# Rotary loads split from their arithmetic, one attention fetch moved ahead of eight loads, and squares moved ahead of evictions in a hybrid decoder block on one core

## The chip, the cores and the metric

The kernel runs on one core of one Trainium2 chip. The metric is the device time of one execution in microseconds (us), as the median of several runs. Trace times count from the start of the span, which is the time from the first to the last instruction of one profiled execution.

The core has five engines with a queue of instructions each: TensorE (PE, matmuls), VectorE (DVE), ScalarE (ACT), GpSimd (POOL) and SyncE (SP, which here only issues loads). An engine works through its queue in order. Transfers go through 16 DMA engines.

## The reference

One decoder layer on a sequence of 1024 tokens, model width 1024, in float32. After a first RMSNorm a wide projection feeds two branches, a gated linear recurrence and a dilated window attention in three groups of four heads. They are merged, projected, normed, and followed by a SwiGLU feed-forward part of width 2816. The parts that the change touches are these:

```python
def rms_norm(x, g):
    y = xf * lax.rsqrt(jnp.mean(xf * xf, axis=-1, keepdims=True) + EPS)
    return (y * g.astype(jnp.float32)).astype(x.dtype)
...
def partial_rope(t, cos, sin):
    half = ROPE_DIM // 2
    t1 = t[..., :half]
    t2 = t[..., half:ROPE_DIM]
    return jnp.concatenate([t1 * cos - t2 * sin, t2 * cos + t1 * sin, t[..., ROPE_DIM:]], axis=-1)
...
    s = jnp.einsum('brnqhc,brnkhc->brnhqk', qb, kb)
    s = jnp.where(mask[None, None, :, None], s, NEG)
    m = jnp.max(s, axis=-1, keepdims=True)
    p = jnp.exp(s - m)
```

The rotary part turns the first 32 of 128 components of each query and key head, for 12 heads.

## The kernel before

**Arithmetic.** A float32 product is made of three matmuls, since each operand is split into a high and a low part: `split` writes the high part on ACT (`whi`, `hth`) and the low part, source minus high, on DVE (`wlo`, `htl`). The large projections save one product in eight by a Strassen-like scheme; a `Quad` makes four 512x512 blocks of a projection from seven products P1 to P7, which are interleaved quad by quad. `Quad.prep` loads a pair of weight tiles (`wraw`, two buffers), forms sums of them on GpSimd (`sa`, `sb`), and splits the first tile, `sa`, `sb`, and a half of the second tile (`w4h`, `w4l`). So the first buffer of a pair comes free early in a quad and the second when `w4l` is done, near its end. P6 and P7 use the split of `sa`.

**Order.** The code of one engine is mostly run in the order in which a scheduler placed it; `tc.issue_after(x)` keeps what stands in it behind x. `load` chains all loads on SP in the order of the program. In the first loop over quads (`q1`: gates, queries and keys, and the gates of the merge) a counter goes up at every step (`tick`), and a table `todo` runs functions at given ticks: sixteen units of the recurrence, from tick 15 on every eight ticks (`lru_a`, and `lru_b` four ticks later), and six rotary units from tick `ROPE0` = 146 on every `ROPED` = 5 ticks. Tiles for both come from the pool `b2`, with 10 buffers of 128x512.

**Start.** `x_load(h, j)` brings x transposed, half h of the tokens, for the products, and `row_load` brings the same rows in the other direction (`xn`), for the sums of squares. `squares` takes them on ACT (`sq`), four tiles for each half. `rates` makes the reciprocal root from them: `rs` on ACT, a few small steps and `dg` on DVE, and one matmul on PE (`prb`) that spreads it. `normed` scales x by it on DVE, in place. Meanwhile the first projection (`v0_mm`, banks `bk0` and `bk1` for the two halves) runs on x that is not yet scaled, and `v0_out` scales its rows when it evicts them on ACT (`vs`). `put` splits a part of x. Then `v_start` and `v_quad` make the other values from the scaled x.

**Rotary.** `rotate(g, u)` loads four tiles of a group and a half of the tokens (`rq1`, `rq2` from the stored queries and keys, `rcs`, `rsn` from the tables), takes four products, a difference and a sum, and stores two tiles from GpSimd. One of the products, `rm2`, is on GpSimd (L812), the rest on DVE.

**Attention start.** `fetch_qk(h, g)` loads the query and key tile of head h and group g. `scores` calls it if it was not called before. In the stretch where attention begins, the results of the recurrence (`ld`) are also loaded, eight tiles `lraw`, to be split into `lTh` (ACT) and `lTl` for the products `py`.

Of the kernel before, what the change touches and what calls it, by code (L numbers as in the profile page):

```python
# [12 lines left out]
OP = mybir.AluOpType  # L13
# [32 lines left out]
ROPE0, ROPED = 146, 5  # L46
# [16 lines left out]
def block(ctx, tc, a, out):  # L63
# [364 lines left out]
    def row_load(t):  # L428
        XN.append(sp.tile([128, 1024], F32, name="xn", bufs=4))
        load(XN[t], a["x"][128 * t:128 * t + 128, :])  # L430
# [5 lines left out]
    def rates(ss):  # L436
# [11 lines left out]
        for t in range(4):  # L448
            V.tensor_scalar(dg[:, t], ident, e[:, t:t + 1], None, op0=OP.mult)
# [46 lines left out]
    for j in range(4):  # L496
        x_load(1, j)
    for t in range(4, NT):
        row_load(t)
    V.tensor_scalar(gneg, gpos, -0.5, None, op0=OP.mult)  # L500
    bk0 = [ps("pv") for _ in range(4)]
    ss = [sp.tile([128, 4], F32, name=f"ss{h}") for h in range(2)]
    for j in range(4):
        if j == 0:
            w0_split(j)
            with tc.issue_after(last_dve[0].ins):
                put(0, j)
        else:
            put(0, j)
            w0_split(j)  # L510
        if j < 3:
            v0_mm(bk0, 0, j)
# [5 lines left out]
    for j in range(4):  # L518
        put(1, j)
    for t in range(4, NT):  # L520
        squares(t, ss[1])
    for j in range(4):
        normed(0, j, rb)
# [3 lines left out]
    v0_out(bk0, 0, r0)  # L527
# [4 lines left out]
    for j in range(4):  # L532
        normed(1, j, rb)
    for j in range(4):
        put(0, j)
# [265 lines left out]

    def rotate(g, u):

        c = slice(512 * u, 512 * u + 512)
        t1, t2, cs, sn, m1, m2 = (b2(n) for n in ("rq1", "rq2", "rcs", "rsn", "rm1", "rm2"))
        rows = [qkd[g, :, :, 16 * i:16 * i + 16, c].rearrange("h s p n -> (h s) p n") for i in range(2)]
        load(t1, rows[0])
        load(t2, rows[1])
        for s, t in ((0, cs), (1, sn)):
            load(t, rtd[g, s, :, c].unsqueeze(0).broadcast_to([8, 16, 512]))  # L810
        V.tensor_mul(m1, t2, sn)
        G.tensor_mul(m2, t1, sn)  # L812
        V.tensor_mul(t1, t1, cs)
        V.tensor_mul(t2, t2, cs)
        V.tensor_sub(t1, t1, m1)
        V.tensor_add(t2, t2, m2)
        G.dma_start(rows[0], t1)
        G.dma_start(rows[1], t2)
# [11 lines left out]
    for n in range(6):  # L830
        todo.setdefault(ROPE0 + ROPED * n, []).append((rotate, (n // 2, n % 2)))
# [287 lines left out]

    for k in range(KT):  # L1120
        load(lraw[k], ld[k])
# [466 lines left out]
```

## Time and profile before

| | |
|---|---|
| runs, median of 3 | 1753.15 us (1753.12 to 1754.28) |
| profiled execution | 1749.78 us |
| its span | 1748.0 us |
| mean granted PE clock | 0.978 of full |
| PE busy | 1676.7 us, 96% of the span |
| DVE busy | 1113.9 us, 64% |
| ACT busy | 727.5 us, 42% |
| POOL busy | 698.0 us, 40% |
| DMA | 262.70 MB, mean 150 GB/s |

The profiled execution is a little longer than its span, by what lies before the first and after the last instruction. Busy times of different engines overlap; an engine's idle time costs something only where the engine that sets the end waits for it. The granted clock is the share of full speed that PE was given; a busy PE at a low clock does less.

### The profile page before, as it was taken

The page shows a single profiled execution, that of the slowest core. Times are in us where ns is not written, and L with a number is a line of the kernel's source. Part 1 is how long each engine was busy: PE and PEld are TensorE (multiplying, and loading weights), DVE is VectorE, ACT ScalarE, POOL GpSimd, SP SyncE. Part 2 cuts the span into 40 slices and gives each one's busy share as a digit, 9 for nine tenths or more (in the row PEclk, how much of TensorE's full clock was granted, in tenths as well). Part 3 has the DMA queues.
Part 4 walks back from the last instruction along what each step waited for, and adds up shares of the span by engine and source line. Part 5 has one row for each costly group of instructions (what it writes and reads, how often), then busy time and mean ns, then how long its engine had stood idle before and what let it go on. Part 6 is the DMA issues. An engine that isn't in the chain of part 4 may idle for free.

```text
span 1748.0 us, 21093 instructions
## 1 busy us (share of the span) xinstructions
PE 1676.7 (96%) x7748; PEld 1376.2 (79%) x7748; DVE 1113.9 (64%) x1585; ACT 727.5 (42%) x1130; POOL 698.0 (40%) x650
## 2 busy tenths in 40 slices
PE   8999999999999988989999999799999999999996
PEld 6897888787877876878888887678888888788885
DVE  6966676778788665563433577755545555649658
ACT  6423367554555522464451345422222222344343
POOL 2003354554445434214334204576556566400103
PEclk9899999999999999999999999899999999999998
DMA  8233433333333455584618742133222222475353
GB/s 319 73 133 113 148 133 124 135 137 129 127 133 133 139 166 179 197 330 155 229 50 304 269 162 84 49 115 133 102 103 91 103 91 103 150 261 198 109 186 121
DMA packets 95919, 262.70 MB, mean 150 GB/s; under 512 B 13768, under 2 KB 22120, under 8 KB 94408
## 3 DMA queue, kind: packets, MB, share of 16 engines
q1 hardware_dynamic: 70352, 182.49, 30.7%
q0 software_dynamic: 20352, 76.21, 11.5%
q10 hardware_dynamic: 5112, 2.66, 0.5%
q8 instruction: 61, 1.00, 0.2%
q14 instruction: 42, 0.34, 0.1%
HBM read 180.86 MB, written 80.35 MB: 149 GB/s over the span
## 4 chain that ended last, share of the span: by engine, by line
PE 77%; DVE 8%; DMA 5%; issue 4%; POOL 3%; ACT 2%; SPq 1%; ACTq 0%; DVEq 0%; POOLq 0%
PE pq L135 14%; PE pq L134 14%; PE pq L133 14%; PE pd L1334 4%; PE pd L1335 4%; PE pd L1333 4%; DMA rsn<-rtd 3%; PE py L135 2%; PE py L134 2%; PE py L133 2%; PE pv L463 2%; PE po L1017 2%; PE pv L133 1%; PE pv L135 1%; PE pv L134 1%
## 5 line engine op out<-in xcount | busy, mean ns | idle before, releaser
L135 PE MATMUL pq<-hth,wlo 128*128 128x512 f32 x448 | 179.7, 401 | 9.8 <-DVE wlo L99 9.8
L133 PE MATMUL pq<-hth,whi 128*128 128x512 f32 x448 | 179.6, 401 | 2.8 <-ACT whi L98 2.8
L134 PE MATMUL pq<-htl,whi 128*128 128x512 f32 x448 | 180.7, 403 | 0.0
L267 POOL TENSOR_TENSOR sb<-wraw 128x512 f32<-128x512 f32 x50 | 71.6, 1432 | 173.1 <-DMA wraw<-in_w_fg 92.3
L98 ACT ACTIVATE whi<-sa 128x1024 fp32r<-128x1024 f32 x50 | 53.0, 1059 | 201.5 <-PE pq L134 126.8
L1334 PE MATMUL pd<-fbl,fah 128*128 128x512 f32 x304 | 119.7, 394 | 4.5 <-DVE fbl L99 4.5
L1335 PE MATMUL pd<-fbh,fal 128*128 128x512 f32 x304 | 119.7, 394 | 0.0
L1333 PE MATMUL pd<-fbh,fah 128*128 128x512 f32 x304 | 119.3, 393 | 0.0
L98 ACT ACTIVATE whi<-wraw 128x1024 fp32r<-128x1024 f32 x67 | 70.7, 1055 | 98.2 <-PE pq L134 25.8
L135 PEld LDWEIGHTS pq<-hth,wlo 128*128 128x128 f32 x448 | 86.0, 192 | 32.1 <-DVE wlo L99 11.6
L99 DVE TENSOR_TENSOR wlo<-wraw,whi 128x1024 fp32r<-128x1024 f32 x67 | 91.6, 1367 | 26.4 <-ACT whi L98 23.7
L309 DVE TENSOR_TENSOR uw<-pq,uw 128x512 f32<-128x512 f32 x100 | 68.3, 683 | 60.2 <-PE pq L135 59.5
L133 PEld LDWEIGHTS pq<-hth,whi 128*128 128x128 f32 x448 | 86.0, 192 | 24.7 <-ACT whi L98 3.2
L134 PEld LDWEIGHTS pq<-htl,whi 128*128 128x128 f32 x448 | 85.9, 192 | 20.5
L1407 POOL TENSOR_TENSOR y<-y,gpf 128x512 f32<-128x512 f32 x16 | 25.2, 1602 | 186.9 <-ACT fah L98 109.5
L99 DVE TENSOR_TENSOR wlo<-sa,whi 128x1024 fp32r<-128x1024 f32 x50 | 70.1, 1401 | 28.6 <-ACT whi L98 28.6
L1239 POOL TENSOR_TENSOR fo<-fo,ut 128x512 f32<-128x512 f32 x44 | 60.6, 1381 | 67.1 <-DVE ut L1238 67.1
L720 DVE TENSOR_TENSOR fb<-pq,uw 128x512 f32<-128x512 f32 x84 | 67.8, 807 | 29.4 <-PE pq L135 29.0
L99 DVE TENSOR_TENSOR fal<-ar,fah 128x1024 fp32r<-128x1024 f32 (+1 forms) x41 | 50.5, 1231 | 51.5 <-ACT fah L98 51.4
L98 ACT ACTIVATE fah<-ar 128x1024 fp32r<-128x1024 f32 (+1 forms) x41 | 40.8, 995 | 100.9 <-PE pd L1334 79.5
L133 PE MATMUL pq<-t1h,whi 128*128 128x512 f32 x200 | 79.6, 398 | 0.9 <-ACT whi L98 0.9
L134 PE MATMUL pq<-t1l,whi 128*128 128x512 f32 x200 | 79.4, 397 | 0.0
(542 smaller groups left out, 4948.0 us busy)
## 6 DMA issues: line engine op xcount, KB each, us to landing
ar<-fd SPq DMA_DIRECT2D x35, 512.0 KB
qkd<-fb POOLq DMA_DIRECT2D x24, 512.0 KB, 3.6
qk<-qkd SPq DMA_DIRECT2D x24, 512.0 KB
wraw<-in_w_fg SPq DMA_DIRECT2D x24, 512.0 KB
wraw<-in_w_fu SPq DMA_DIRECT2D x24, 512.0 KB
fd<-fo POOLq DMA_DIRECT2D x11, 1024.0 KB, 4.3
wd<-in_w_dn SPq DMA_DIRECT2D x21, 512.0 KB
fd<-fs POOLq DMA_DIRECT2D x11, 768.0 KB, 5.6
```

What stands on the lines that cost most here:

```text
L98: A.activation(hi, src, AF.Copy)
L99: (le or V).tensor_sub(lo, src, f(hi))
L133: T.matmul(o, lh, rh, start=(first and i == 0), stop=False)
L134: T.matmul(o, lh, rl, start=False, stop=False)
L135: T.matmul(o, ll, rh, start=False, stop=(last and i == n - 1))
L267: G.tensor_add(sb[:, lo_], r1[:, lo_], r1[:, hi_])
L309: V.tensor_add(y, bank, x)
L720: V.tensor_add(o, half_in(bank, g), half_in(add, g))
L1239: G.tensor_mul(g, g, ut)
L1333: T.matmul(o, ah[:, ts], bh, start=(i == 0), stop=False)
L1334: T.matmul(o, ah[:, ts], bl, start=False, stop=False)
L1335: T.matmul(o, al[:, ts], bh, start=False, stop=(i == NP - 1))
```

## The change

There are three parts. In the start, the last two x loads of the second half stand behind the last four row loads, the second half's `squares` stand ahead of two of its four `put`, and `v0_out` of the first half is kept behind the second half's `rs`. In the first loop, `rotate` is split: `rotate_load` issues the four loads one unit, 5 ticks, ahead of the arithmetic; `ROPE0` goes from 146 to 148, so that loads stand at ticks 143, 148, ... 168 and the arithmetic at 148, 153, ... 173, where both stood at 146, 151, ... 171; and `m2` is on DVE. In the attention start, `fetch_qk(0, 2)` is called ahead of the eight `lraw` loads.

```diff
-ROPE0, ROPED = 146, 5
+ROPE0, ROPED = 148, 5
...
-            V.tensor_scalar(dg[:, t], ident, e[:, t:t + 1], None, op0=OP.mult)
+            last_dve[0] = V.tensor_scalar(dg[:, t], ident, e[:, t:t + 1], None, op0=OP.mult)
...
-    for j in range(4):
+    for j in range(2):
         x_load(1, j)
     for t in range(4, NT):
         row_load(t)
+    for j in range(2, 4):
+        x_load(1, j)
...
-            put(0, j)
-            w0_split(j)
+            with tc.issue_after(last_dve[0].ins):
+                put(0, j)
+                w0_split(j)
...
-    for j in range(4):
+    for j in range(2):
         put(1, j)
     for t in range(4, NT):
         squares(t, ss[1])
+    with tc.issue_after(last_act[0].ins):
+        for j in range(2, 4):
+            put(1, j)
     for j in range(4):
         normed(0, j, rb)
     bk1 = [ps("pv") for _ in range(4)]
     v0_mm(bk1, 1, 0)
     r1, rb = rates(ss[1])
-    v0_out(bk0, 0, r0)
+    with tc.issue_after(last_act[0].ins):
+        v0_out(bk0, 0, r0)
...
-    for j in range(4):
-        normed(1, j, rb)
-    for j in range(4):
-        put(0, j)
+    with tc.issue_after(last_dve[0].ins):
+        for j in range(4):
+            normed(1, j, rb)
+        for j in range(4):
+            put(0, j)
...
+    def rotate_load(g, u):
+
+        c = slice(512 * u, 512 * u + 512)
+        t = RT[g, u] = [b2(n) for n in ("rq1", "rq2", "rcs", "rsn")]
+        for i in range(2):
+            load(t[i], qkd[g, :, :, 16 * i:16 * i + 16, c].rearrange("h s p n -> (h s) p n"))
+        for i in range(2):
+            load(t[2 + i], rtd[g, i, :, c].unsqueeze(0).broadcast_to([8, 16, 512]))
+
     def rotate(g, u):
...
+        t1, t2, cs, sn = RT.pop((g, u))
+        m1, m2 = b2("rm1"), b2("rm2")
         V.tensor_mul(m1, t2, sn)
-        G.tensor_mul(m2, t1, sn)
+        V.tensor_mul(m2, t1, sn)
...
     for n in range(6):
+        todo.setdefault(ROPE0 + ROPED * (n - 1), []).append((rotate_load, (n // 2, n % 2)))
         todo.setdefault(ROPE0 + ROPED * n, []).append((rotate, (n // 2, n % 2)))
...
+    fetch_qk(0, 2)
     for k in range(KT):
         load(lraw[k], ld[k])
```

The order of ACT at the start, from the first half's `rs` on. `sq` are the squares, `vs` the evictions of the first half, `hth` the copies of `put`. Before:

```order
L425 ACTIVATE hth1_121<-x_125 128x2x512
L479 ACTIVATE vs0_393<-pv_167,rr4_287 128x512
L434 ACTIVATE sq_333,ss1_172<-xn_158 128x1024
L479 ACTIVATE vs0_393<-pv_168,rr4_287 128x512
L434 ACTIVATE sq_335,ss1_172<-xn_160 128x1024
L479 ACTIVATE vs0_393<-pv_169,rr4_287 128x512
L434 ACTIVATE sq_337,ss1_172<-xn_162 128x1024
L479 ACTIVATE vs0_393<-pv_170,rr4_287 128x512
L434 ACTIVATE sq_339,ss1_172<-xn_164 128x1024
L425 ACTIVATE hth0_120<-x_128 128x2x512
L439 ACTIVATE rs4_377<-ss1_172,epsc_87 128x4
```

After the change:

```order
L434 ACTIVATE sq_329,ss1_172<-xn_156 128x1024
L434 ACTIVATE sq_331,ss1_172<-xn_158 128x1024
L425 ACTIVATE hth0_120<-x_128 128x2x512
L434 ACTIVATE sq_333,ss1_172<-xn_160 128x1024
L425 ACTIVATE hth0_120<-x_129 128x2x512
L434 ACTIVATE sq_335,ss1_172<-xn_162 128x1024
L425 ACTIVATE hth1_121<-x_124 128x2x512
L439 ACTIVATE rs4_377<-ss1_172,epsc_87 128x4
L479 ACTIVATE vs0_393<-pv_167,rr4_287 128x512
L425 ACTIVATE hth1_121<-x_125 128x2x512
```

The evictions moved behind `rs`, and two `hth` copies of the scaled first half (x_128, x_129) stand between the squares.

The order of SP in the first rotary quads: `wraw` are a quad's two weight tiles, the four tiles from `rq1` to `rsn` a rotary unit. Before:

```order
L109 DMA wraw_4993<-in_w_g 128x1024
L109 DMA wraw_4995<-in_w_g 128x1024
L109 DMA rq1_5034<-qkd_1410 128x1x512
...
L109 DMA rsn_5037<-rtd_117 128x1x512
L109 DMA rq1_5144<-qkd_1410 128x1x512
...
L109 DMA rsn_5147<-rtd_117 128x1x512
L109 DMA wraw_5166<-in_w_g 128x1024
L109 DMA wraw_5168<-in_w_g 128x1024
L109 DMA rq1_5254<-qkd_1410 128x1x512
```

After the change:

```order
L109 DMA rq1_4961<-qkd_1410 128x1x512
...
L109 DMA rsn_4964<-rtd_117 128x1x512
L109 DMA wraw_5001<-in_w_g 128x1024
L109 DMA wraw_5003<-in_w_g 128x1024
L109 DMA rq1_5082<-qkd_1410 128x1x512
...
L109 DMA rsn_5085<-rtd_117 128x1x512
L109 DMA wraw_5156<-in_w_g 128x1024
L109 DMA wraw_5158<-in_w_g 128x1024
L109 DMA rq1_5207<-qkd_1410 128x1x512
```

The first unit moved ahead of a pair of weight tiles, the second behind it; the third stands behind the next pair in both, now with the fourth unit behind it.

The order of DVE in the second of these quads, from the low part of its first weight tile to that of `sa`. Before:

```order
L99 TENSOR_TENSOR wlo_5177<-wraw_5166,whi_5176 128x1024
L811 TENSOR_TENSOR rm1_5258<-rq2_5255,rsn_5257 128x512
L309 TENSOR_TENSOR uw_5205<-pq_5192,p1_5142 128x512
L813 TENSOR_TENSOR rq1_5254<-rq1_5254,rcs_5256 128x512
...
L816 TENSOR_TENSOR rq2_5255<-rq2_5255,rm2_5259 128x512
L309 TENSOR_TENSOR uw_5220<-pq_5207,uw_5205 128x512
L720 TENSOR_TENSOR fb_5162<-pq_5222,uw_5220 128x512
L99 TENSOR_TENSOR wlo_5181<-sa_5170,whi_5180 128x1024
```

After the change:

```order
L99 TENSOR_TENSOR wlo_5167<-wraw_5156,whi_5166 128x1024
L825 TENSOR_TENSOR rm1_5307<-rq2_5208,rsn_5210 128x512
L309 TENSOR_TENSOR uw_5195<-pq_5182,p1_5150 128x512
L826 TENSOR_TENSOR rm2_5308<-rq1_5207,rsn_5210 128x512
...
L830 TENSOR_TENSOR rq2_5208<-rq2_5208,rm2_5308 128x512
L728 TENSOR_TENSOR fb_5152<-pq_5230,uw_5228 128x512
L825 TENSOR_TENSOR rm1_5417<-rq2_5318,rsn_5320 128x512
L99 TENSOR_TENSOR wlo_5171<-sa_5160,whi_5170 128x1024
```

The third unit stands at the same place; the product of GpSimd joined it, and the first product of the fourth unit stands ahead of `wlo` of `sa`.

## Rows read from the trace of the kernel before

**Rows 1.** The page's first part: busy us, share of the span, instructions.
```profile
PE 1676.7 (96%) x7748; PEld 1376.2 (79%) x7748; DVE 1113.9 (64%) x1585; ACT 727.5 (42%) x1130; POOL 698.0 (40%) x650
```

**Rows 2.** Windows of 10 us: busy us and instructions by engine, clock, DMA share, GB/s.
```profile
30.00:40.00 10.00, 9.79 (x43) 7.59 (x41) 7.76 (x11) 7.86 (x15) 1.66 (x2) 1.00 0.59 231
40.00:50.00 10.00, 3.26 (x6) 1.96 (x7) 7.77 (x16) 3.62 (x4) 0.00 (x0) 0.62 0.55 191
```

**Rows 3.** Timeline of PE: start, duration, instruction, idle before it and releaser.
```profile
27.64 1.02 PE L451 MATMUL prb<-dg,ones 128*128 128x512 f32 x2
...
46.74 2.04 PE L451 MATMUL prb<-dg,ones 128*128 128x512 f32 x2 [6.95 <-DVE dg L449]
...
78.45 0.28 PE L133 MATMUL pv<-whi,hth 128*128 128x256 f32 x1
```

**Rows 4.** Timeline of ACT at the start.
```profile
32.14 0.69 ACT L479 ACTIVATE vs<-pv,rr 128x512 f32<-128x512 f32 x1 [5.28 <-PE pv L463]
32.73 1.05 ACT L434 ACTIVATE sq<-xn 128x1024 f32<-128x1024 f32 x1
...
39.55 0.29 ACT L439 ACTIVATE rs<-ss,epsc 128x4 f32<-128x4 f32 x1
```

**Rows 5.** Timeline of DVE at the start.
```profile
45.73 0.86 DVE L449 TENSOR_SCALAR dg<-cst,re 128x128 f32<-128x128 f32 x4
48.82 5.36 DVE L457 SCALAR_TENSOR_TENSOR x<-x,gneg,prb 128x512 f32<-128x512 f32 x8 [2.23 <-PE prb L451]
...
74.44 1.21 DVE L550 TENSOR_TENSOR htl<-x,hth 128x1024 fp32r<-128x1024 f32 x1
75.58 1.21 DVE L621 TENSOR_TENSOR wlo<-wraw,whi 128x1024 fp32r<-128x1024 f32 x1
```

**Rows 6.** Waits of DVE, 600 to 700 us: total, times, longest.
```profile
DVE rm L811 <- DMA rsn<-rtd: 36.3, 6, 9.0
```

**Rows 7.** Waits of PE, 600 to 700 us: total, times, longest.
```profile
PE pq L135 <- DVE wlo L99: 9.8, 4, 4.7
```

**Rows 8.** Timeline of DVE in the rotary stretch.
```profile
612.88 0.69 DVE L811 TENSOR_TENSOR rm<-rq,rsn 128x512 f32<-128x512 f32 x1 [6.37 <-DMA rsn<-rtd]
...
620.27 0.69 DVE L811 TENSOR_TENSOR rm<-rq,rsn 128x512 f32<-128x512 f32 x1 [2.40 <-DMA rsn<-rtd]
...
641.72 1.82 DVE L811 TENSOR_TENSOR rm<-rq,rsn 128x512 f32<-128x512 f32 x1 [9.04 <-DMA rsn<-rtd]
...
647.87 1.21 DVE L99 TENSOR_TENSOR wlo<-sa,whi 128x1024 fp32r<-128x1024 f32 x1
```

**Rows 9.** Timeline of PE in the rotary stretch.
```profile
649.13 0.80 PE L135 MATMUL pq<-hth,wlo 128*128 128x512 f32 x1 [4.68 <-DVE wlo L99]
649.73 0.63 PE L133 MATMUL pq<-hth,whi 128*128 128x512 f32 x1
...
653.14 0.53 PE L135 MATMUL pq<-hth,wlo 128*128 128x512 f32 x1
...
674.56 0.79 PE L135 MATMUL pq<-hth,wlo 128*128 128x512 f32 x1 [3.68 <-DVE wlo L99]
```

**Rows 10.** Timeline of SP's DMA issues in the rotary stretch.
```profile
612.94 16.14 SPq L109 DMA_DIRECT2D wraw<-in_w_g  x2
629.25 1.29 SPq L109 DMA_DIRECT2D rq<-qkd  x2
```

**Rows 11.** Line L812 by itself: count, shortest, median and longest ns, first and last start.
```profile
L812 POOL TENSOR_TENSOR rm<-rq,rsn x6: 1291/1760/1811, 612.9 to 691.0; 128x512 f32<-128x512 f32 x6
```

**Rows 12.** Timeline of PE at the attention start.
```profile
762.71 0.55 PE L901 MATMUL psc<-qk 128*128 128x128 f32 x1 [5.53 <-DMA qk<-qkd]
```

**Rows 13.** Timeline of SP's DMA issues at the attention start.
```profile
740.19 10.59 SPq L109 DMA_DIRECT2D lraw<-ld  x8
750.82 0.93 SPq L109 DMA_DIRECT2D qk<-qkd  x2
```

More of the change, by code (lines that the diff above doesn't have):

```diff
@@ L800, in lru_b @@
         G.dma_start(ld[cb, :, 512 * u:512 * u + 512], i)
-    def rotate(g, u):
[L804 to L810, printed above, removed]
+    RT = {}
+    def rotate_load(g, u):
[5 more added lines that the diff above has]
+            load(t[2 + i], rtd[g, i, :, c].unsqueeze(0).broadcast_to([8, 16, 512]))
+    def rotate(g, u):
+        t1, t2, cs, sn = RT.pop((g, u))
+        m1, m2 = b2("rm1"), b2("rm2")
         V.tensor_mul(m1, t2, sn)
-        G.tensor_mul(m2, t1, sn)
+        V.tensor_mul(m2, t1, sn)
         V.tensor_mul(t1, t1, cs)
@@ L816, in rotate @@
         V.tensor_add(t2, t2, m2)
-        G.dma_start(rows[0], t1)
-        G.dma_start(rows[1], t2)
+        c = slice(512 * u, 512 * u + 512)
+        for i, t in enumerate((t1, t2)):
+            G.dma_start(qkd[g, :, :, 16 * i:16 * i + 16, c].rearrange("h s p n -> (h s) p n"), t)
     def late_rates():
```

## The prediction

> **What bounds the kernel now.** I read the page first: TensorE (PE) is busy for 1676.7 of 1748.0 us [rows 1], so only what stops PE, or slows its clock, costs time. I then looked for the stops in the three stretches that the change touches, with the PE timeline, the chain of waits by engine, and the timeline of the engine that PE waited for.
>
> In the first 80 us the reader is to see one stop: PE stands 6.95 us before the second `prb` matmul, for VectorE's (DVE's) `dg` [rows 3]. The chain behind it starts on ScalarE (ACT): the `vs` evictions wait 5.28 us for PE, the four `sq` of the second half stand among them, and `rs` comes at 39.55 [rows 4]; on DVE `dg` ends at 46.59 [rows 5]. After the stop PE runs slow: in the window 40 to 50 us the granted clock is 0.62, with PE busy 3.26 us, against 43 matmuls in the 10 us before, 0.23 us each, at full clock [rows 2].
>
> In the rotary stretch (600 to 700 us) DVE waits 36.3 us, six times, for the sine table `rsn` of a rotary unit [rows 6], and PE waits 9.8 us, four times, for the `wlo` that stands behind this on DVE [rows 7]. Only the second number costs time, with what the clock loses behind it: after the stop of 4.68 us nine matmuls (649.73 to 653.14) start 0.43 apart instead of 0.23 [rows 9], so the clock is at half, and some 2.0 us are lost with the one before them; after the stop of 3.68 I put 2.8. So some 14.6 us hang on the rotary part.
>
> In the attention start PE waits 5.53 us for the `qk` tile of head 0, group 2 [rows 12], whose loads SyncE (SP) issues at 750.82, behind eight `lraw` loads issued from 740.19 for 10.59 us [rows 13].
>
> **Start-up.** The squares move ahead of the evictions, so `rs` and `dg` no longer wait for PE. By the order on ACT the last `sq` now follows two `put` copies that need DVE's first four `normed` steps, so `rates(1)` is not free at once. With 1.05 us per ACT pass of 128x1024 [rows 4] and DVE's unchanged `normed` steps I place the second `prb` at about 40, where PE has just finished what it had (about 39.6): the wait of 6.95 nearly goes. With the slow clock behind it (`prb` 2.04 against 1.02 the first time [rows 3], some eight matmuls by 0.2 as in [rows 9]) PE gains about 9.6 us up to there.
> But DVE does not gain as much. From `prb` on it has eight `normed` steps (5.36 us [rows 5]), then, by the order, 21 passes of 128x1024 at 1.14 us (74.44 to 75.58 [rows 5]) and two of 0.6 before the `wlo` for `v_quad`'s first product is done: 31.6 us, against 28.0 before (48.82 to 76.79 [rows 5]), since three `htl` and one `wlo` that stood ahead of `dg` now stand behind it. From 41 that ends at 72.6. PE began this product at 78.45 [rows 3]. It would be there at about 69.5, so a new wait of some 3 us opens, and with it a slow stretch of about 1.5 us, as behind the other stops. Six matmuls of 256 columns, 0.12 us each as half of the 0.23, go ahead of the wait. Net: 78.45 - 72.6 + 0.7 - 1.5 = 5.0 us gained. Bounds: 9.6 if DVE's passes prove to have slack, 3.0 if `prb` comes 2 us later. I take **5.0**: the DVE passes stand end to end in this stretch, so their sum counts.
>
> **The moved x loads.** Two x loads go behind four `xn` loads. The transfers are the same; the two x tiles are needed later than the squares now. Nothing, covered by the passes above.
>
> **Rotary.** Three things change. The product `m2` moves from GpSimd (1.29 to 1.81 us, median 1.76 [rows 11]) to DVE (0.69 us, as its twin at 612.88 [rows 8]): six times 0.6 us more on DVE, but the detour over GpSimd goes, worth about 1.1 us per unit that stands on the path. The arithmetic comes two ticks later, the loads three ticks earlier.
> What counts is where loads and arithmetic stand now. On SP each unit's four loads still come in line with the `wraw` pairs; before the change two `wraw` issue from 612.94 for 16.14 us (the second waits for its buffer until the quad's end) and the unit's loads come right behind, at 629.25 [rows 10], so that `rsn` serves DVE at 641.72, 12.5 us later [rows 8]. By the order of the changed kernel, unit 0 alone gets ahead of its `wraw` pair. Units 1, 2, 4 and 5 are still issued right behind a second `wraw`, and on DVE their first product still stands right behind the next `wlo`. These waits of DVE stay. What goes is the second unit inside a quad: before the change unit 1 is waited for again at 620.27, 2.40 us [rows 8], which pushes everything behind it, and with it the next second `wraw`. So I walk through the quads:
> - First (unit 1 alone): no stop. Its tail is about 4.5 us earlier, so the next second `wraw` is issued near 624.5 instead of 629.
> - Second (units 2 and 3): unit 2's `rsn` lands near 637.5, its arithmetic ends near 641; unit 3 lands some 6 us behind it. `wlo` of `sa` at about 645 instead of 647.87 [rows 8], where PE needs it at 644.2 (649.13 less 4.68 [rows 9], less the 0.2 of the first quad). Stop about 1 instead of 4.68, no slow clock.
> - Third (unit 4 alone): PE is here some 6.5 us earlier, DVE's wait for unit 4 only 3: stop about 3 instead of 3.68, slow stretch 2 to 2.7.
> - Fourth (unit 5): stop about 1.5, as before.
> Sum: 5.5 us of stops and 2.6 of slow clock are left of 14.6: **6.5** gained. Bounds: 14.6 if the waits fall away altogether, 0 or a little under if unit 3's landing just takes over the stop at `sa` (then 2.5 with what the third quad saves).
>
> How long a unit takes to land decides this. The row is 12.5 us from issue to use [rows 8, 10]. The Trainium skill, page "DMA: Bandwidth & Descriptors", section "Anatomy of one DMA — SWDGE (gpsimd) path", gives about 2.0 us plus the bytes over 436 GB/s, for transfers that GpSimd issues. By it the second `wraw` and a unit, 1.5 MB, would land in an estimated 5.6 us, DVE would hardly wait, and the sum would be that of the first rival below, about 1734. The trace disagrees by a factor of two for these loads.
>
> **Attention.** The two `qk` loads of group 2 now stand ahead of the eight `lraw`; their buffers come free with the first scores of head 0, near 743. So the wait of 5.53 goes from there. But the `lraw` loads start 3 us later than 740.19 and have 1 MB ahead of them, and by the order on ACT three of the eight `lTh` copies, instead of one, now stand behind the softmax of the first groups. PE runs the scores early and then stands before the products of the last `lTh`. I take **0.5 lost**; bounds 6 gained (the wait and its slow clock go whole) and 3 lost (the delay of `lraw` shows whole).
>
> **Sum.** 5.0 + 6.5 - 0.5 = 11.0 us of the span of 1748.0, so 1737.0. The profiled execution took 1749.78, and the median of the runs, 1753.15, is 3.4 above that; the difference is taken over: **1742.2**. No change means within 0.2%, 3.5 us.
>
> **The rivals.**
> - *Rotary loads really lead* (0.14). Every unit's data is there when DVE comes. For it: that is what an issue five ticks ahead does if a tick is long. Against: the order on SP, where the second `wraw` is still the gate. 14.6 + 5.0 - 0.5: 1734.
> - *DVE is not the next limit at the start* (0.13): the 9.6 us stay whole. For it: GpSimd and ACT could be late too, and DVE's work need not be in time everywhere. Against: DVE's passes without a gap. 15.6 gained: 1737.5.
> - *The rotary change does nothing* (0.15): the loads move with the arithmetic, the same waits end last, only one unit later. Left are 5.0 - 0.5: 1748.7.
> - *Slower* (0.06): SP, which issues in order, stands at a unit's loads for a buffer (a unit takes four of a pool of ten, and its two temporaries come on top), and the `wraw` pair behind it is late. Place: units 1, 3 and 5. Each us past the time at which the second `wraw` was free to go is a us for PE. At 4.5 us in three quads it costs 13.5, less 4.5: 1762. It decides from 1.5 us a quad. Against: four, two and four fit into ten, and the tiles freed are those of work some 20 us old.
> - *Little anywhere* (0.04): rotary as the third, and `prb` late: about 1751.
>
> **How the numbers follow.** The forecast has 0.48. Faster by over 0.2%: 0.48 + 0.14 + 0.13 and two thirds of the third rival, 0.85. Within 0.2%: the rest of that and the last, 0.09. Slower: 0.06. The range goes from the first rival, 1733, to a little past the third, 1750.
>
> **What would show it.** Right: the second `prb` near 40 with hardly a wait, and a new wait for `wlo` near 70; DVE waits of 6 to 9 us for `rsn` for units 1, 2, 4, 5; PE stops of about 1, 3 and 1.5 us in quads two to four; no wait for `qk` of group 2, but waits for `lTh` behind it. Wrong: no new wait near 70, or `rsn` not among DVE's waits (then nearer 1734), or SP late at `wraw` (then slower).

## The result and the profile after

The changed kernel takes 1736.59 us (median of 4 runs, 1734.92 to 1740.01) against 1753.72 us for the kernel before, measured beside it (4 runs, 1753.12 to 1761.02): ratio 0.9897, 95% interval 0.987 to 0.9923. It is faster, by 1.0%. The forecast was 1742.2, with a range of 1733 to 1750. The profiled execution took 1737.8 us with a span of 1736.0; the span was forecast as 1737.0. So the span's difference, 12.0 us against the 11.0 forecast, was closer than the medians' difference, 17.1 us: the profiled execution of before lay 3.4 below the median of its three runs, that of the changed kernel 1.2 above its own, and I had carried the 3.4 over as if it belonged to the kernel. By the medians alone the two faster rivals, 1734 and 1737.5, came nearer than the forecast; only the traces can tell which mechanism was at work.

The page's first part after the change; PE has the same work in a shorter span:

```profile
PE 1676.3 (97%) x7748; PEld 1376.8 (79%) x7748; DVE 1121.0 (65%) x1591; ACT 728.4 (42%) x1130; POOL 693.2 (40%) x644
```

To see where the 12 us came from I set each matmul of one trace beside the same matmul of the other and took the difference of their starts. A matmul that starts 5.5 us earlier at 590 us tells that 5.5 us were won up to there; it stands as -5.5. All times at the head of a column are those of the kernel before; the entries are the difference at that matmul.

| span's differences to the kernel before, us | 60 | 590 | 705 | 800 | 1734 |
|---|---|---|---|---|---|
| changed kernel | -11.7 | -5.5 | -16.2 | -12.4 | -12.0 |

So the start-up wins 11.7 and gives 6.2 of it back, the rotary stretch wins 10.6, and the attention start gives 3.7 back (16.13 at 735 to 12.42 at 800). Other executions of the same code give other numbers, as the experiments show below.

**Start-up.** The windows of 10 us (compare [rows 2]): the hole between 40 and 50 us is gone, at full clock, and a smaller one opens behind 60, with the granted clock at 0.83 behind it.

```profile
40.00:50.00 10.00, 10.00 (x45) 8.02 (x44) 10.00 (x13) 1.10 (x2) 0.00 (x0) 1.00 0.22 70
50.00:60.00 10.00, 10.00 (x64) 9.01 (x63) 10.00 (x9) 6.29 (x8) 1.45 (x2) 1.00 0.42 150
60.00:70.00 10.00, 7.85 (x65) 7.43 (x63) 9.79 (x11) 8.85 (x12) 0.09 (x1) 1.00 0.17 58
70.00:80.00 10.00, 9.20 (x64) 9.20 (x65) 8.80 (x10) 2.00 (x2) 0.70 (x1) 0.83 0.35 107
```

PE's timeline (compare [rows 3]): the second `prb` waits 0.69 us at 37.78 instead of 6.95 at 46.74. New waits of 1.76 and 1.19 us stand before `v_quad`'s first product.

```profile
9.99 2.03 PE L463 MATMUL pv<-wlo,hth 128*128 128x512 f32 x8
...
37.78 1.10 PE L451 MATMUL prb<-dg,ones 128*128 128x512 f32 x2 [0.69 <-DVE dg L449]
...
69.09 0.51 PE L133 MATMUL pv<-whi,hth 128*128 128x256 f32 x2 [1.76 <-ACT whi L628]
70.80 0.39 PE L134 MATMUL pv<-wlo,hth 128*128 128x256 f32 x1 [1.19 <-DVE wlo L629]
```

The first of these rows shows what I had not forecast: the kernel before waited here, in the row that the next fence quotes from its PE timeline, for DVE's first `wlo`. In the changed kernel that matmul runs at 9.99 without a wait.

```profile
12.18 2.07 PE L463 MATMUL pv<-wlo,hth 128*128 128x512 f32 x7 [2.09 <-DVE wlo L420]
```

On DVE (compare [rows 5]) the chain behind `prb` stands end to end, as forecast, and its `wlo` ends at 70.75:

```profile
38.92 5.36 DVE L457 SCALAR_TENSOR_TENSOR x<-x,gneg,prb 128x512 f32<-128x512 f32 x8
...
69.53 1.22 DVE L629 TENSOR_TENSOR wlo<-wraw,whi 128x1024 fp32r<-128x1024 f32 x1
```

**Rotary.** The waits of DVE (580 to 700 us) and of PE (590 to 700 us), total, times, longest (compare [rows 6, 7]): DVE still waits nearly as long for `rsn`, and PE stops once, for 3.1 us, instead of four times for 9.8.

```profile
DVE rm L825 <- DMA rsn<-rtd: 32.2, 5, 9.8
```

```profile
PE pq L135 <- DVE wlo L99: 3.1, 1, 3.1
```

PE's timeline at this stop shows what it costs besides: eight matmuls, from 661.98 to 664.96, start 0.43 us apart instead of 0.23, so the clock is at half for them, and some 1.6 us go to it.

```profile
661.17 0.50 PE L135 MATMUL pq<-hth,wlo 128*128 128x512 f32 x1 [3.14 <-DVE wlo L99]
...
661.98 0.63 PE L135 MATMUL pq<-hth,wlo 128*128 128x512 f32 x1
662.40 0.63 PE L133 MATMUL pq<-hth,whi 128*128 128x512 f32 x1
...
665.38 0.40 PE L134 MATMUL pq<-t1l,whi 128*128 128x512 f32 x1
```

DVE's timeline (compare [rows 8]) has the waits of units 1, 2, 3 and 4, and `wlo` of `sa` behind them:

```profile
606.66 0.83 DVE L825 TENSOR_TENSOR rm<-rq,rsn 128x512 f32<-128x512 f32 x1 [5.67 <-DMA rsn<-rtd]
...
627.84 0.69 DVE L825 TENSOR_TENSOR rm<-rq,rsn 128x512 f32<-128x512 f32 x1 [7.24 <-DMA rsn<-rtd]
...
634.58 0.69 DVE L825 TENSOR_TENSOR rm<-rq,rsn 128x512 f32<-128x512 f32 x1 [1.24 <-DMA rsn<-rtd]
635.18 1.22 DVE L99 TENSOR_TENSOR wlo<-sa,whi 128x1024 fp32r<-128x1024 f32 x1
...
654.49 0.69 DVE L825 TENSOR_TENSOR rm<-rq,rsn 128x512 f32<-128x512 f32 x1 [9.81 <-DMA rsn<-rtd]
```

The issues of SP (compare [rows 10]) show the same pattern as before, a unit right behind the second weight tile, but the second tile goes 10.36 us after the first instead of 16.14:

```profile
606.97 10.36 SPq L109 DMA_DIRECT2D wraw<-in_w_g  x2
617.43 1.24 SPq L109 DMA_DIRECT2D rq<-qkd  x2
```

From its issue at 617.43 to its use at 627.84 unit 2 takes 10.4 us, less than the 12.5 us of the kernel before. The estimate of 5.6 us, worked out from the Trainium skill's page "DMA: Bandwidth & Descriptors" (section "Anatomy of one DMA — SWDGE (gpsimd) path", for transfers that GpSimd issues), is again too short for these loads, which SP issues.

**Attention start.** The wait of 5.53 us [rows 12] is gone; PE stops four times instead, for 7.5 us by these rows of its timeline. Behind the last of them the product of the softmax (`po`) waits 0.41 us more for `pts`, the transposed probabilities that ACT copies.

```profile
747.72 0.50 PE L134 MATMUL py<-lTl,whi 128*128 128x512 f32 x1 [1.72 <-DVE lTl L99]
749.18 0.50 PE L134 MATMUL py<-lTl,whi 128*128 128x512 f32 x1 [0.50 <-DVE lTl L99]
...
756.39 0.50 PE L133 MATMUL py<-lTh,whi 128*128 128x512 f32 x1 [2.07 <-ACT lTh L98]
...
767.21 1.54 PE L917 MATMUL psc<-qk 128*128 128x128 f32 x8 [3.18 <-DMA qk<-qkd]
```

SP (compare [rows 13]) issues the moved fetch at 727.31 and the `lraw` loads behind it from 728.16. The kernel before issued them at 740.19, which less the 16.1 us won by then is 724.1: they start 4.1 us late.

### The profile page after: what moved, and what is told of

The parts are those of the page before. It is cut to its first block, busy times and chain, and to the rows that moved or that the text cites. A ratio compares the mean times of both kernels' runs of the same rounds, so it can differ in the third digit from the quotient of the medians.

```text
span 1736.0 us, 21088 instructions
## 1 busy us (share of the span) xinstructions
PE 1676.3 (97%) x7748; PEld 1376.8 (79%) x7748; DVE 1121.0 (65%) x1591; ACT 728.4 (42%) x1130; POOL 693.2 (40%) x644
## 4 chain that ended last, share of the span: by engine, by line
PE 77%; DVE 10%; DMA 4%; issue 4%; POOL 3%; ACT 3%; SPq 0%; ACTq 0%; DVEq 0%; POOLq 0%
PE pq L135 15%; PE pq L134 15%; PE pq L133 15%; PE pd L1351 4%; PE pd L1352 4%; PE pd L1350 4%; PE py L135 2%; PE py L133 2%; PE py L134 2%; PE pv L463 2%; PE po L1033 2%; PE pv L134 1%; PE pv L135 1%; DMA rsn<-rtd 1%; PE pv L133 1%
## 5 line engine op out<-in xcount | busy, mean ns | idle before, releaser
L99 DVE TENSOR_TENSOR wlo<-wraw,whi 128x1024 fp32r<-128x1024 f32 x67 | 97.5, 1456 | 23.6 <-ACT whi L98 20.8
L268 POOL TENSOR_TENSOR sa<-sb,wraw 128x512 f32<-128x512 f32 x50 | 80.2, 1604 | 0.0
```

The costliest lines, as they stand in the source:

```text
L99: (le or V).tensor_sub(lo, src, f(hi))
L268: G.tensor_sub(sa[:, lo_], sb[:, lo_], r0[:, lo_])
```

## The experiments

Each is named by its label. "Without the fetch" is the changed kernel without its attention fetch (`no_fetch`), the base of most of them. The table has the same differences as above, to the kernel before, in each kernel's profiled execution, and the ratio of the times measured.

| kernel | 590 | 705 | 735 | 800 | 1734 | ratio to before (95%) |
|---|---|---|---|---|---|---|
| start_only | -7.9 | -7.1 | -7.0 | -6.8 | -4.2 | 0.9968 (0.995 to 0.9986) |
| rotary_only | +1.0 | -7.1 | -7.1 | -6.4 | -8.1 | 0.9925 (0.9906 to 0.9945) |
| fetch_only | +0.9 | +1.5 | +1.6 | +4.8 | +5.6 | 1.0011 (0.9997 to 1.0024) |
| no_fetch | -6.1 | -16.7 | -16.7 | -16.6 | -18.4 | 0.9896 (0.9871 to 0.992) |
| m2_pool | -4.8 | -12.1 | -12.1 | -11.4 | -10.9 | 0.9893 (0.9862 to 0.9925) |
| no_lead | -6.0 | -12.9 | -12.9 | -11.7 | -8.8 | 0.9904 (0.9878 to 0.9931) |
| early_phase | -4.3 | -10.5 | -10.5 | -4.4 | -3.2 | 0.9927 (0.9907 to 0.9946) |
| lead_far | -3.6 | -6.7 | -6.7 | -4.4 | -5.8 | 0.9927 (0.9901 to 0.9954) |
| far_room | -5.9 | -21.4 | -21.4 | -21.4 | -21.9 | 0.9868 (0.9847 to 0.989) |
| fetch_mid | -8.1 | -15.6 | -15.6 | -12.1 | -10.8 | 0.9894 (0.9866 to 0.9922) |
| mid_early | -7.9 | -15.9 | -15.9 | -6.2 | -6.9 | 0.9934 (0.9917 to 0.9952) |
| old_split_order | -1.6 | -12.7 | -12.7 | -12.8 | -11.7 | 0.9925 (0.9906 to 0.9943) |

How far such an entry can be trusted is seen where kernels have the same program. Ten of them, the changed kernel and all rows but `rotary_only`, `fetch_only` and `old_split_order`, are alike up to 577 us, and they stand at -3.6 to -8.1 at 590. The changed kernel, `no_fetch`, `fetch_mid` and `mid_early` are alike up to 705, where they stand at -15.6 to -16.7; but from 590 to 705 they win 10.6, 10.6, 7.5 and 8.0, and `old_split_order` and `rotary_only`, with the same rotary part, 11.1 and 8.1. So executions of the same code differ by up to 4.5 us in the start and by 3.6 us in the rotary stretch, and each entry is one execution: a smaller difference between two kernels is not shown by this table. The single runs of the kernel before range from 1748.87 to 1759.27 in one group of 23.

### The three parts alone, and without the fetch

`start_only` has the start-up hunks of the diff, `rotary_only` the rotary ones, `fetch_only` the one line below, and `no_fetch` all but this line.

```diff
+    fetch_qk(0, 2)
     for k in range(KT):
         load(lraw[k], ld[k])
```

Expected of start_only: 

> The kernel before with the start-up part of the change alone (x loads, put and weight split order, squares ahead of evictions). Theory A, the parts add up as the aligned traces have it: the matmuls of the recurrent stretch (130 to 560 us) stand 5.8 us earlier, and with rotary and attention as before nothing is given back, so the span is 5.8 shorter, near 1742, and the ratio to before about 0.9965. Rival B, the stretch at the attention start is limited by its transfers and eats what is won ahead of it: 2 us or less are left at the end, though the 5.8 show at 560 us.

Expected of rotary_only: 

> The kernel before with the rotary part alone (loads one unit ahead, m2 on VectorE, start at tick 148). Theory A: 10.3 us of the span, as between 560 and 700 us in the aligned traces: about 1737.7, ratio 0.994; VectorE still waits 5 to 10 us for rsn before units 1, 2, 4 and 5. Rival B: 10.3 at 700 us, but 6 or less at the end. A further rival (the changed phase against the start made it): gain between 4 and 8 already at 700 us.

Expected of fetch_only: 

> The kernel before with the attention fetch alone ahead of the eight lraw loads. Theory A: the wait of 5.5 us for qk of group 2 goes, but the lraw loads start some 4 us later and waits for lTh, lTl and a later qk take its place: 3 to 4 us slower at the end, span near 1751.7. My prediction's own value was 0.5 slower. Rival B: no change within 1 us, since the same transfers bound the stretch in both orders.

Expected of no_fetch: 

> The changed kernel without its attention fetch (start-up and rotary parts together). Theory A: the 3.8 us that the changed kernel gives back between 765 and 790 us are not given back: span near 1732, 4 us faster than the changed kernel. Rival B: the same as the changed kernel, about 1736, with waits of PE at the attention start that sum to as much.

Measured: the start alone is 0.32% faster, the rotary part alone 0.75%. In the traces they win 7.1 us each up to 705; both together, in four executions, 15.6 to 16.7. So the parts add up within the scatter, and the times say the same: 0.9968 times 0.9925 is 0.9893, and both together measured 0.9896. The 7.1 us of the rotary part alone (8.1 from its own 590 on) are less than the 10.3 of theory A and lie in or at the edge of the 4 to 8 of the further rival; with 7.5 to 11.1 us in six executions of this rotary part the run decides nothing between them. Rival B, that the attention start eats what is won ahead of it, falls: `start_only` keeps 6.8 of 7.0 across it, and `no_fetch` 16.6 of 16.7. The fetch alone loses 3.2 us in its stretch (735 to 800), and in the changed kernel 3.7, by the trace. The kernels without it lose 2.3 us or less there, but for `early_phase`, which loses 6. The ratio measured for the fetch alone, 1.0011, has an interval that just takes in no change, so the loss of 3 us stands on the traces of three executions (with `fetch_mid` below), not on the times; nor do the times tell the changed kernel (0.9897) from `no_fetch` (0.9896). The 2.6 us that `start_only` has less at the end than at 800 come from stretches that the change doesn't touch.

PE's timeline of `no_fetch` at the attention start shows both waits of the kernel before again, and yet nothing lost:

```profile
745.72 3.76 PE L917 MATMUL psc<-qk 128*128 128x128 f32 x16 [5.26 <-DMA qk<-qkd]
...
765.40 1.13 PE L917 MATMUL psc<-qk 128*128 128x128 f32 x8 [1.06 <-DMA qk<-qkd]
```

### The parts of the rotary change

`m2_pool` puts the product `m2` back on GpSimd, `no_lead` issues a unit's loads in the tick of its arithmetic, `early_phase` keeps lead and product and goes back to tick 146.

```diff
m2_pool
-        V.tensor_mul(m2, t1, sn)
+        G.tensor_mul(m2, t1, sn)
no_lead
-        todo.setdefault(ROPE0 + ROPED * (n - 1), []).append((rotate_load, (n // 2, n % 2)))
+        todo.setdefault(ROPE0 + ROPED * n, []).append((rotate_load, (n // 2, n % 2)))
early_phase
-ROPE0, ROPED = 148, 5
+ROPE0, ROPED = 146, 5
```

Expected of m2_pool: 

> Start-up and rotary parts without the fetch, with the product m2 back on GpSimd. Theory A, the rotary gain comes from taking the second unit out of a quad, and m2 on VectorE adds about 1.1 us for each unit on the path: 2 to 4 us of the 10 between 560 and 700 us go, span some 2 to 4 longer than without the fetch. Rival: VectorE's move off GpSimd is the main part of the rotary gain: 6 us or more go. Other rival: GpSimd's product was hidden, under 1 us.

Expected of no_lead: 

> Start-up and rotary parts without the fetch, but the four loads of a unit in the same tick as its arithmetic (148, 153, ...), so nothing is issued ahead; m2 stays on VectorE. Theory A, loads and arithmetic only counted by where they stand in a quad: the lead is worth what the first unit's move ahead saves, and 5 or more of the 10 us between 560 and 700 us go. Rival, the lead does nothing since the waits for rsn stay for four of six units: the rotary stretch is as with the lead within 1.5 us.

Expected of early_phase: 

> Start-up and rotary parts without the fetch, with ROPE0 back at 146 (loads at 141, 146, ..., arithmetic at 146, 151, ...), so lead and m2 on VectorE stay and only the phase against the quads changes. By m2 (3.5 to 3.9 us) and the lead (2.2 to 4.4 us) some 2.5 of the 10 us of the rotary stretch are left for the phase: 1.5 to 3.5 us slower there. Rival, the phase does nothing (within 1 us) and the parts don't add.

Measured at 705, against 15.6 to 16.7: 12.1, 12.9 and 10.5. Read so, going without m2 on VectorE would cost 3.5 to 4.6 us, as expected, without the lead 2.7 to 3.8, less than the 5 of theory A, and without the phase 5.1 to 6.2, about twice what I expected. But part of this lies ahead of the rotary stretch. From 590 to 705 alone the three win 7.3, 6.9 and 6.2 us, against 7.5 to 11.1 with all three edits, so no cost of a single edit stands clear of the scatter. Nor do the times tell `m2_pool` (0.9893) and `no_lead` (0.9904) from `no_fetch` (0.9896). What the traces do show is that PE stops for `wlo` once, for 2.7 to 5.2 us, in the six executions with all three edits, and twice or three times with one of them missing. The waits of PE in the stretch 560 to 705 us (total, times, longest) in `m2_pool`, `no_lead` and `early_phase`:

```profile
PE pq L135 <- DVE wlo L99: 5.4, 2, 4.2
```

```profile
PE pq L135 <- DVE wlo L99: 5.8, 2, 5.2
```

```profile
PE pq L135 <- DVE wlo L99: 7.0, 3, 4.4
```

In `early_phase` SP also stands once for 11.2 us (580 to 700 us) at a unit's loads, until a unit's stores have left their buffers: what the prediction's rival "slower" describes, at a lead of five ticks. The kernel loses another 6 us between 735 and 800, with PE waiting 6.3 us for `qk` and 2.7 us for `pts`; what its phase changes there I did not follow.

### A longer lead, without and with room

`lead_far` loads nine ticks ahead of the arithmetic. `far_room` does too, writes `m2` over `rsn`, gives the pool one buffer more, and lets `rcs` and `rsn` take their buffers ahead of `rq1` and `rq2`.

```diff
lead_far, far_room
-ROPE0, ROPED = 148, 5
+ROPE0, ROPED = 150, 5
...
-        todo.setdefault(ROPE0 + ROPED * (n - 1), []).append((rotate_load, (n // 2, n % 2)))
+        todo.setdefault(ROPE0 + ROPED * (n - 1) - 4, []).append((rotate_load, (n // 2, n % 2)))
far_room
-B2 = 10
+B2 = 11
...
-        t = RT[g, u] = [b2(n) for n in ("rq1", "rq2", "rcs", "rsn")]
+        t = [b2(n) for n in ("rcs", "rsn", "rq1", "rq2")]
+        t = RT[g, u] = t[2:] + t[:2]
...
-        m1, m2 = b2("rm1"), b2("rm2")
+        m1, m2 = b2("rm1"), sn
```

Expected of lead_far: 

> Start-up and rotary parts without the fetch, with the loads nine ticks ahead of the arithmetic (141, 146, ... and 150, 155, ...) instead of five, so that a unit stands ahead of the pair of weight loads behind which it stood. Theory A, VectorE's remaining waits for rsn (32 us) are there because a unit is issued behind the second weight load of the quad in which it is used: they fall under 8 us, and the 3 to 4 us that PE still loses in the stretch go. Rival, SyncE stands at a unit's loads for buffers and the weight pair behind it comes late: the stretch is 2 us or more slower.

Expected of far_room: 

> As lead_far (loads nine ticks ahead), but with room: m2 is written over rsn, so that a unit needs five buffers instead of six, the pool has 11 instead of 10, and rcs and rsn take their buffers first. Theory A, lead_far lost 9 us in the rotary stretch because its temporaries and loads waited for the stores of the unit before (16.9 us of waits of VectorE for qkd<-rq), not because of the lead: these waits fall under 6 us, rsn is not waited for, and the stretch from 560 to 700 us is 2 to 4 us shorter than without the fetch at a lead of five. Rival, the pair of weight loads behind two units on SyncE comes late whatever the room: the stretch stays 5 us or more longer.

Measured: `lead_far` has no wait for `rsn` left, and stands 9 to 10 us later at 705 than the kernels with a lead of five, of which 2 to 4.5 lay ahead of 590 already; from 590 on it wins 3.2 us. DVE waits instead, for the stores of the unit before, since the buffers of its temporaries are still being stored (waits of DVE in `lead_far`, 560 to 700 us):

```profile
DVE rm L825 <- DMA qkd<-rq: 16.9, 2, 8.5
DVE rm L825 <- issue: 8.2, 1, 8.2
```

In `far_room` both are gone, and its remaining waits are those of a DVE that is done early (same view):

```profile
DVE fb L728 <- issue: 15.8, 4, 4.4
DVE uw L309 <- PE pq L135: 10.0, 6, 2.7
```

PE doesn't wait for `wlo` in this stretch at all, and the matmuls at 705 stand 21.4 us earlier than before, 4.7 to 5.8 more than in the changed kernel and its like. Theory A is borne out: with the room, the same lead wins 15.6 us from 590 to 705, well above the 7.5 to 11.1 at a lead of five, and as much as the 14.6 of the kernel before that I had put down to rotary waits. Which of its three edits makes the room was not taken apart, and both kernels also stand two ticks later (150 instead of 148), which no run has alone. At 1729.76 us (1728.15 to 1735.75) it has the lowest median of all kernels here. Its interval reaches to 0.989, and those of the changed kernel and of `no_fetch` begin at 0.987 and 0.9871, so the step from 0.9897 to 0.9868 is shown by the traces, and likely by the times.

### The place of the fetch

`fetch_mid` puts the fetch between the fourth and the fifth `lraw` load, where SP waits anyway. `mid_early` moreover writes the last four splits ahead of the first attention steps.

```diff
fetch_mid, mid_early
-    for k in range(KT):
+    for k in range(4):
+        load(lraw[k], ld[k])
+    fetch_qk(0, 2)
+    for k in range(4, KT):
         load(lraw[k], ld[k])
...
mid_early
-    after(-2)
     for k in range(4, KT):
         split(lraw[k], lTh[k], lTl[k])
+    after(-2)
     after(-1)
```

Expected of fetch_mid: 

> Start-up and rotary parts, with the fetch of head 0's group 2 between the fourth and the fifth lraw load instead of ahead of the first. Theory A, the fetch costs because it delays the first lraw loads by some 4 us, while SyncE waits anyway before the fifth: the wait of 5.5 us for qk goes, lraw stays in time, 4 to 7 us faster than without the fetch, span near 1725. Rival, the stretch is bound by its transfers (410 GB/s for 25 us): nothing is won, within 1.5 us of the kernel without the fetch.

Expected of mid_early: 

> As fetch_mid, with the copies of the last four lraw tiles ahead of the first softmax steps in the program, so that no lTh stands behind an exponential on ScalarE. Theory A, the fetch gives its 7 us back because two lTh copies stand behind the exponentials and make PE wait for lTh (2.7 us) and for pts (2.5 us): both waits go and the kernel is 3 to 6 us faster than without the fetch from 775 us on. Rival B, the stretch is bound by the softmax of head 0, whose first exponential starts no earlier: within 2 us of the kernel without the fetch, with other waits of PE in their place; or slower, as the exponentials start later.

Measured: both theories A fell. In `fetch_mid` the `lraw` loads are in time and the wait for group 2 is gone (SP's issues and PE's timeline):

```profile
724.64 1.74 SPq L109 DMA_DIRECT2D lraw<-ld  x4
727.89 0.80 SPq L109 DMA_DIRECT2D qk<-qkd  x2
733.48 1.75 SPq L109 DMA_DIRECT2D lraw<-ld  x4
```

```profile
754.01 0.50 PE L133 MATMUL py<-lTh,whi 128*128 128x512 f32 x1 [2.70 <-ACT lTh L98]
...
765.80 1.13 PE L917 MATMUL psc<-qk 128*128 128x128 f32 x8 [1.19 <-DMA qk<-qkd]
...
775.63 2.08 PE L1033 MATMUL po<-pts,vt 128*128 128x128 f32 x8 [2.52 <-ACT pts L1023]
```

Yet by the trace it loses 3.5 us from 735 to 800, as much as the changed kernel (the times, 0.9894, don't tell it from `no_fetch`). So the fetch costs time where the `lraw` loads are in time, too. The two kernels lose it at different waits. Set beside `no_fetch`, the changed kernel is 0.3 us ahead at 764 us and 3.5 behind at 772, by its wait of 3.18 for the `qk` of head 1's group 1 and the slow clock after it. `fetch_mid` is 0.4 behind at 772 and 4.6 at 780, by its wait of 2.52 for `pts` and the slow clock after that.

What holds `pts` can be read from ACT and DVE. In `no_fetch`:

```profile
768.65 1.37 DVE L99 TENSOR_TENSOR wlo<-wraw,whi 128x1024 fp32r<-128x1024 f32 x1
770.60 0.40 ACT L938 ACTIVATE pb<-pb,st 128x128 f32<-128x128 f32 x1 [2.02 <-DVE st L933]
771.84 1.08 ACT L1023 ACTIVATE pts<-ppt 128x512 f32<-128x512 f32 x2
```

In `fetch_mid`:

```profile
769.88 1.23 DVE L99 TENSOR_TENSOR wlo<-wraw,whi 128x1024 fp32r<-128x1024 f32 x1 [2.40 <-ACT whi L98]
772.90 0.40 ACT L938 ACTIVATE pb<-pb,st 128x128 f32<-128x128 f32 x1 [2.57 <-DVE st L933]
775.00 1.06 ACT L1023 ACTIVATE pts<-ppt 128x512 f32<-128x512 f32 x2
```

PE begins the transposes `ppt` of head 0 at nearly the same time in both (771.14 and 771.55), but on ACT the copies `pts` stand behind exponentials (`pb`) of head 1's group 1, and these wait for `st`, which DVE makes from the maxima of their scores. In `fetch_mid` five exponentials instead of three stand ahead, and on DVE a `wlo` of the projection stands ahead of the last four maxima, where it waits for ACT; in `no_fetch` it stands behind three of the four and does not wait. So by these rows the order on ACT and DVE, which moved with the fetch, makes `pts` late, and not the softmax of head 0 itself. No run changed this order alone. In the changed kernel `pts` starts at 776.20, behind six exponentials that wait 3.32 us for `st`. The rival of the run, bound by transfers at 410 GB/s, does not fit either: the changed kernel moves 389 GB/s over its busiest 25 us (729 to 754), and the stretch became longer, not equal.

In `mid_early` all `lTh` stand ahead of the exponentials of head 0's group 1. The first of these starts at 752.23, against 747.95 in `fetch_mid`, waiting for DVE's `st`, and 9.7 us are lost; PE's waits in 725 to 800 us:

```profile
PE po L1033 <- ACT pts L1023: 6.2, 1, 6.2
PE psc L917 <- DVE mix L1132: 5.9, 1, 5.9
```

The second row is the scores of head 1's group 1, late behind a product of DVE (`mix`). Behind them the pattern is the same, with `pts` at 779.95 behind five exponentials that wait longer for `st`:

```profile
777.85 0.40 ACT L938 ACTIVATE pb<-pb,st 128x128 f32<-128x128 f32 x1 [5.61 <-DVE st L933]
```

So the kernel got slower, as rival B allowed (0.9934, against 0.9896 of `no_fetch`), but that the softmax of head 0 is the bound is not shown.

### The order at the very start

`old_split_order` is without the fetch and takes back one hunk, the `issue_after` around `put` and `w0_split`.

```diff
-            with tc.issue_after(last_dve[0].ins):
-                put(0, j)
-                w0_split(j)
+            put(0, j)
+            w0_split(j)
```

Expected of old_split_order: 

> Start-up and rotary parts without the fetch, with put and the weight split of the second to fourth unit in the old order (no issue_after there). Theory A, the 2.2 us that the changed kernel gains at 12 us come from this edit alone, since it lets the first weight's low part go ahead of the second htl on VectorE: the wait of 2.09 us is back. At 130 us 1 to 2.5 us of it are left, as VectorE's chain behind the second prb starts 2.2 later. Rival, the chain behind prb starts by ScalarE's squares and not by this: no difference at 130 us within 0.7.

Measured: PE's wait is back, as theory A has it, and 4.4 us are lost up to 590, more than the 1 to 2.5 expected. PE's timeline, and its window from 10 to 20 us:

```profile
12.21 2.94 PE L463 MATMUL pv<-wlo,hth 128*128 128x512 f32 x8 [2.06 <-DVE wlo L420]
```

```profile
10.00:20.00 10.00, 7.94 (x27) 6.01 (x27) 10.00 (x10) 5.21 (x7) 9.11 (x6) 0.83 1.03 404
```

The clock fell behind the wait in this execution, 0.83, which costs another 2 us; the kernel before has the same wait, and in its profiled execution the clock stayed at 1.00 there:

```profile
10.00:20.00 10.00, 7.91 (x33) 5.88 (x33) 10.00 (x10) 5.26 (x7) 9.12 (x6) 1.00 1.03 404
```

So this hunk is worth its wait of 2.1 us, and about twice that where the clock falls behind it. The whole start-up part won 3.6 to 8.1 us at 590 in ten executions; without this hunk 1.6 are left, in one. The other edits of the start were not run apart.

## Why the prediction was right, step by step

**What bounds.** Right: PE's stops are where the time came from. Over the whole span its idle time fell from 71.3 to 59.7 us, and its busy time, in which the slow clock would show, hardly changed (1676.7 to 1676.3).

**Start-up, 5.0 forecast, 5.5 in the profiled execution**, 3.6 to 8.1 in ten. The size was right and part of the reason was missing. The mechanism I named was there: `prb` without its wait (0.69 left), and a new wait of "some 3 us" near 70, for DVE's chain (1.76 and 1.19 at 69.09 and 70.80). So the rival that DVE is not the next limit fell: of 11.7 us at 60, 6.2 are left at 130. The chain's terms as I listed them add up to 30.5 us, not to the 31.6 that I wrote; from the first `normed` to the end of `wlo` it took 31.8 (38.92 to 70.75). But I placed `prb` at 40 and it came at 37.78, since the matmuls ahead of it ran 2.2 us earlier. That was the wait of 2.09 at 12.18, which stood in the timeline of before, and I had given the new order of `put` and `w0_split` no term of its own. `old_split_order` shows what it was worth: without it, 1.6 us of the start-up's gain are left. So this size came out near the forecast partly by luck.

**Rotary, 6.5 forecast, 10.6 in the trace** (8.1 in `rotary_only`). The walk through the quads had the mechanism: DVE's waits for `rsn` stay (32.2 of 36.3 us), the second unit inside a quad goes, the loads behind the next second `wraw` are issued earlier (617.4, which is 622.9 in the time of the kernel before, instead of 629; I had put 624.5), no stop in the first quad and one of 3 us in the third (3.14 measured), with slow matmuls behind it (1.6 us, forecast 2 to 2.7). What was mis-sized are the stops of the second and the fourth quad: I left 1 and 1.5 us, and there were none. In the second quad the term is unit 2's landing: I put it at 637.5, and DVE used it at 627.84, or 633.3 in the time of the kernel before, as it came 10.4 us after its issue and not 12.5. And part of the 10.6 is luck: `fetch_mid` and `mid_early`, with the same program up to there, stop 5.2 and 4.6 us in the third quad with slow matmuls behind, and win 7.5 and 8.0 us, nearer to the forecast. PE's waits in `fetch_mid`, 560 to 705 us:

```profile
PE pq L135 <- DVE wlo L99: 5.2, 1, 5.2
```

**Attention, 0.5 lost forecast, 3.7 measured**, beyond my bound of 3. This step failed. I named the late `lraw` loads and the `lTh` copies behind the exponentials as what takes the place of the wait for `qk`. `fetch_mid` shows that late loads are not needed for the loss: with them in time it is the same by the trace. And none of the kernels that end this wait gains by it: in the changed kernel the products behind it stand 6.9 us ahead of those of `no_fetch` at first, and by 764 only 0.3. What PE waits for instead is the next `qk` and `pts`, which stands on ACT behind exponentials of the next head. Which order on ACT and DVE would give the time back stays open; `mid_early`, my attempt, made it worse.

**The sum** of 11.0 came out as 12.0 in the spans, with rotary 4.1 better, the attention 3.2 worse, and the start 0.5 better: two errors of opposite sign, so that the sum came out near is luck, the more so as executions of the same code differ by as much. The rival "the rotary change does nothing" fell with the 8.1 us of `rotary_only`. The rival "rotary loads really lead" did not happen here, and the reason given against it, the second `wraw` as the gate, was right, as `far_room` fits: with a lead that goes ahead of that gate, and with room, the rotary stops are gone. The rival "slower", where a unit's loads and temporaries wait for buffers, did not happen in the changed kernel, and did at a lead of nine ticks (`lead_far`).

## What to carry to other kernels

Read a wait as lost time only if nothing behind it ends later: closing PE's 5.3 us wait for `qk` moved it to other places, while the stops in the rotary stretch were worth all they took. When loads are moved ahead, look at the instruction that holds the queue in front of them and at the buffers that they take; between 590 and 705 us the lead of nine ticks with room won 15.6 us, without it 3.2, and the lead of five 7.5 to 11.1. And set the same instruction of both traces side by side, for equal programs too: these differed by up to 4.5 us in one stretch, which tells how small a difference may still be read from one trace.

## What the runs showed of the hardware

A stop of the same length doesn't always cost the same, even in the same program. The ten kernels with the same start all wait 1.76 us at about 69 us and 1.2 us at about 71. Behind these waits, from 70 to 80 us, the granted clock, as the mean of a window with stretches at full and at half clock, was 1.00 in three of them (`start_only`, `fetch_mid`, `mid_early`), 0.83 in five (the changed kernel, whose row stands above, `no_fetch`, `m2_pool`, `no_lead`, `far_room`), and 0.68 and 0.66 in `early_phase` and `lead_far`. At 130 us they stand 8.1 to 8.2, 6.1 to 6.7, and 5.1 to 5.6 us ahead of the kernel before. The window in `start_only` and in `early_phase`:

```profile
70.00:80.00 10.00, 9.08 (x77) 9.08 (x78) 10.00 (x11) 2.11 (x3) 0.79 (x1) 1.00 0.35 107
```

```profile
70.00:80.00 10.00, 9.06 (x56) 9.06 (x57) 8.03 (x9) 1.91 (x3) 0.79 (x1) 0.68 0.35 107
```

So most of what these ten differ by in the start is the clock. In the same way the wait of 2.1 us at 12 us was followed by full clock in the profiled execution of before (1.00 from 10 to 20 us) and by 0.83 in those of `rotary_only` and `fetch_only`, which have the same program up to there and stand 1.0 and 0.9 us behind it at 590. The Trainium skill's page "TensorE: Matmul & The Clock Gate", section "What's actually happening", says that the gate watches activity on a schedule of its own, which does not begin with the kernel, so that one kernel loses different numbers of slow matmuls from run to run; the windows above agree with that. For this kernel it is a likely part of why single runs spread over 10 us, though no run here took the other parts apart.
